# Turning the softmax weights of a sliding-window attention step in six 128-row blocks instead of eight

## The chip, the cores and the metric

The kernel runs on one core of one Trainium2 chip. The core has a matrix engine (TensorE, PE in the profile; its weight loads are listed apart as PEld), a vector engine (VectorE, DVE), a scalar engine (ScalarE, ACT), a general engine (GpSimd, POOL), queues that start transfers (SyncE, SP, and GpSimd's own), an on-chip memory of 128 partitions (SBUF) and accumulators for matrix products (PSUM, eight banks of 512 float32 per partition). Each engine takes its instructions in the order of its own list, and waits at an instruction until the others have signalled that its inputs are there. The metric is the device time of one execution in microseconds.

## The reference

One block of a streaming encoder: 1024 tokens of width 1024, in float32. A normed input is projected to queries, keys, values and several gates. Branch A is attention over a window of whole 64-token chunks, branch B a gated MLP; both are gated, summed and projected. What the change touches is the attention:

```python
# 16 query heads, 2 key heads, head width 64, chunks of 64 tokens
kb = concatenate([kc[:, j:j + nc] for j in range(3)], axis=2)   # a chunk sees its own and the two chunks before: 192 keys
s = einsum('bnqhgd,bnkhd->bhgnqk', qc, kb) * HEAD_DIM ** -0.5
s = where(valid, s, -1e30)
m = maximum(max(s, -1), sink)
p = exp(s - m)
denom = sum(p, -1) + exp(sink - m)                              # a learned sink per head
o = einsum('bhgnqk,bnkhd->bnqhgd', p / denom, vb)
```

The products are carried out on values split into a high and a low part (hi and lo), so that a product of two float32 matrices is three products of the parts.

## The kernel before, in words

Nearly all of the time goes to large products of 128x128 weights with 512 columns, written as a two-by-two scheme with seven products per pair of output blocks (`gemm_pair`, with the products issued at L338). A pair runs 7 x 12 matmuls; the weights of the next products are cast and split by ScalarE (L152) and VectorE (L153) in the meantime (`split_next`).

The attention has no time of its own. It is a generator (`attention`) of 32 steps: 2 key heads x 8 tiles of 128 tokens x 2 (`par`, the even or odd heads of the group's eight). After every product of the pairs that follow (`part_of_attention`, a hook) one piece of it is written into the program; the Tile scheduler then decides where each instruction stands in its engine's list. In the profile the steps lie between about 340 and 625 us.

A token tile holds two chunks, c = 0 and 1. Its keys are a block of 256: the 128 of the tile before and its own 128. Chunk 0 sees columns 0 to 191 of that block, chunk 1 columns 64 to 255. The four heads of a step are worked as two pairs (i = 0, 1), with the two heads' 64 queries in one set of 128 partitions. A step has three parts, issued in an interleaved way with those of other steps:

- `softmax_stage`: scores on PE (L1075) into one PSUM bank per chunk, their minimum on VectorE (L1083, L1084; scores carry a minus sign), the exponential on ScalarE into the tile `pr` (L1086), the sums' reciprocal (L1095 to L1099), and the scaling of the weights, chunk 0 on VectorE (L1105), chunk 1 on ScalarE (L1107).
- `weight_stage`, two steps later: the weights `pr` (queries on partitions) are turned by PE with the identity, so that the keys lie on partitions. For each of the four (c, i) the first 128 keys of the chunk's window go into one bank (L1127), then for each of the four its last 64 keys into another (L1138, 64 partitions). ScalarE copies a bank's high part (L152) and VectorE subtracts for the low part (L153): the first bank becomes `pT`, with high and low part side by side; the second becomes `pTb`, with the high part on partitions 0 to 63 and the low part on 64 to 127.
- `value_stage`, three steps after the softmax: the products with the values (L1160), per chunk two with `pT` and one with `pTb`, into a bank of kind `ps_o`; ScalarE copies (L1166) and VectorE adds (L1167) the halves into the tile `aT`, which is stored.

PSUM has four kinds of banks with two banks each: `ps_mm` and `ps_o` for the large products (`ps_o` also for the values), `ps_sc` for the scores and `ps_tp` for what is turned. The two banks of `ps_tp` are used in turn, so that a step's second bank can be written when the step before has read its own.

The values of a token tile are loaded by `value_loads` on SP's queue: two transfers (L988) bring the first 128 keys of each chunk's window into `va`, and two more (L991) the last 64 keys of both windows into `vb`, twice, since the high and the low part of the weights both need them. In the first token tile no keys lie before; it has its own case throughout.

Of the kernel before, what the change touches and what calls it, by code (L numbers as in the profile page):

```python
# [24 lines left out]
F32 = mybir.dt.float32  # L25
F32R = mybir.dt.float32r
# [4 lines left out]
P = 128  # L31
# [3 lines left out]
HALF = 512  # L35
# [17 lines left out]
def hybrid_tile(  # L53
# [16 lines left out]
    nc = tc.nc  # L70
# [8 lines left out]
    def nm(s):  # L79
        count[0] += 1  # L80
        return f"{s}_{count[0]}"

    def bank(tag, dt=F32):
        return psum.tile([P, 512], dt, name=nm("ps_" + tag), tag="ps_" + tag, bufs=2)

    def mtile(shape, dt, tag, bufs, pool=None):
        return (pool or main).tile(shape, dt, name=nm(tag), tag=tag, bufs=bufs)
# [13 lines left out]
    ident = const.tile([P, P], F32, name="ident")  # L101
# [43 lines left out]
    def split(hi, lo, src, minus=False):  # L145
        if minus:
            nc.scalar.mul(hi, src, -1.0)
            nc.vector.scalar_tensor_tensor(
                lo, src, -1.0, hi.bitcast(F32), op0=ALU.mult, op1=ALU.subtract
            )  # L150
        else:
            nc.scalar.copy(hi, src)  # L152
            return nc.vector.tensor_sub(lo, src, hi.bitcast(F32))  # L153
# [808 lines left out]
    keys = {}  # L962
# [10 lines left out]
    def value_loads(g, t):  # L973

        va = mtile([P, 2, 3 * HD], F32R, "v", 2, aheads)
        rows = v_dr[:].rearrange("n p g d -> (n p) g d")[:, g, :]
        if t == 0:
            for e in range(2):  # L980
                nc.sync.dma_start(va[e * 64 : (e + 1) * 64, 0, :].bitcast(F32), rows[0:64])
            nc.sync.dma_start(va[:, 1, :].bitcast(F32), rows[0:P])
            keys[g, t][1:3] = (None, va[:, 1, :]), (va[:, 0, :], None)
            return
        vb = mtile([P, 2, 3 * HD], F32R, "vb", 2, pool)
        for c in range(2):
            k = (t - 1) * P + 64 * c
            nc.sync.dma_start(va[:, c, :].bitcast(F32), rows[k : k + P])  # L988
        own = rows[t * P : (t + 1) * P].rearrange("(c p) d -> p c d", c=2)
        for e in range(2):  # L990
            nc.sync.dma_start(vb[e * 64 : (e + 1) * 64].bitcast(F32), own)  # L991
        keys[g, t][1:3] = (va[:, 0, :], va[:, 1, :]), (vb[:, 0, :], vb[:, 1, :])

    def query_stage(g, t, par):
        if par == 0:
# [57 lines left out]
    def atile(shape, dt, tag, bufs):  # L1053
        return mtile(shape, dt, tag, bufs, pool)

    def window_of(t, c):

        return (64 * c, 64 * c + 192) if t else (P, P + 64 * (c + 1))

    def softmax_stage(g, t, par, qt):  # L1060

        kt = keys[g, t][0]
        q_of = qt[:].rearrange("p i (q c) -> p c (i q)", c=2)
        k0 = 0 if t else P
        nmax = atile([P, 2, 2], F32, "sm", 12)
        sums = atile([P, 2, 2], F32, "sm", 12)
        pr = atile([P, 2, 2, 192], F32, "pr", 2)
        sinks_of = (v[:, 4 * g + par : 4 * g + par + 3 : 2] for v in (sink_sb, nsink_sb))
        sk, nsk = sinks_of
        for c in range(2):  # L1070
            lo, hi = window_of(t, c)
            sc = bank("sc")[:].rearrange("p (i k) -> p i k", i=2)
            for i in range(2):
                for f in range(2):
                    nc.tensor.matmul(  # L1075
                        sc[:, i, k0:],
                        q_of[:, c, i * P : (i + 1) * P],
                        kt[:, f, k0:],
                        start=f == 0,
                        stop=f == 1,  # L1080
                    )

            nc.vector.tensor_reduce(nmax[:, c, :], sc[:, :, lo:hi], axis=mybir.AxisListType.X, op=ALU.min)  # L1083
            nc.vector.tensor_tensor(nmax[:, c, :], nmax[:, c, :], nsk, op=ALU.min)  # L1084
            for i in range(2):
                nc.scalar.activation(  # L1086
                    pr[:, c, i, 0 : hi - lo],
                    sc[:, i, lo:hi],
                    AF.Exp,
                    bias=nmax[:, c, i : i + 1],  # L1090
                    scale=-1.0,
                    accum_out=sums[:, c, i : i + 1],
                )
        es = atile([P, 2, 2], F32, "sm", 12)
        nc.vector.tensor_add(es[:], sk.unsqueeze(1).broadcast_to([P, 2, 2]), nmax[:])  # L1095
        exps.append(nc.scalar.activation(es[:], es[:], AF.Exp))
        nc.vector.tensor_add(es[:], es[:], sums[:])
        inv = atile([P, 2, 2], F32, "sm", 12)
        nc.vector.reciprocal(inv[:], es[:])  # L1099
        for c in range(2):  # L1100
            lo, hi = window_of(t, c)
            for i in range(2):
                v = pr[:, c, i, 0 : hi - lo]
                if c == 0:
                    nc.vector.tensor_scalar_mul(v, v, inv[:, c, i : i + 1])  # L1105
                else:
                    nc.scalar.mul(v, v, inv[:, c, i : i + 1])  # L1107
        return pr

    def weight_stage(g, t, par, pr):  # L1110

        _, va, vb, _ = keys[g, t]

        def cols(c):
            return slice(256 * c, 256 * c + 256)

        a = b = None
        chunks = [c for c in range(2) if va[c] is not None]  # L1120
        if chunks:
            used = slice(256 * chunks[0], 512)
            pt = bank("tp")
            for c in chunks:
                for i in range(2):
                    at = (2 * c + i) * P
                    nc.tensor.transpose(pt[:, at : at + P], pr[:, c, i, 0:P], ident[:])  # L1127
            a = atile([P, 2, HALF], F32R, "pT", 2)
            split(a[:, 0, used], a[:, 1, used], pt[:, used])
        chunks = [c for c in range(2) if vb[c] is not None]  # L1130
        if chunks:
            used = slice(0, 256 * (chunks[-1] + 1))
            first = P if t else 0
            pt = bank("tp")
            for c in chunks:
                for i in range(2):
                    at = (2 * c + i) * P
                    nc.tensor.transpose(pt[0:64, at : at + P], pr[:, c, i, first : first + 64], ident[:])  # L1138
            b = atile([P, HALF], F32R, "pTb", 2)
            split(b[0:64, used], b[64:P, used], pt[0:64, used])  # L1140
        return a, b

    def value_stage(g, t, par, parts):


        if par == 0:
            keys[g, t][3] = atile([P, 4, P], F32, "aT", 2)
        _, va, vb, at = keys[g, t]
        a, b = parts
        po = bank("o")  # L1150
        vs = slice(par * HD, par * HD + P)
        for c in range(2):
            cs = slice(256 * c, 256 * c + 256)
            terms = []
            if va[c] is not None:
                terms += [(va[c][:, vs], a[:, n, cs]) for n in range(2)]
            if vb[c] is not None:
                terms.append((vb[c][:, vs], b[:, cs]))
            for n, (lt, rt) in enumerate(terms):
                nc.tensor.matmul(po[:, cs], lt, rt, start=n == 0, stop=n == len(terms) - 1)  # L1160
        here, there = slice(HD * par, HD * (par + 1)), slice(HD * (1 - par), HD * (2 - par))
        out_of, dst = (
            lambda half: po[half].rearrange("p (c i q) -> p c i q", c=2, i=4),
            at[here].rearrange("p i (c q) -> p c i q", c=2),
        )
        nc.scalar.copy(dst, out_of(there))  # L1166
        nc.vector.tensor_add(dst, dst, out_of(here))  # L1167
        if par == 1:
            nc.gpsimd.dma_start(
                at_dr[:].rearrange("(c p) t -> p c t", p=P)[:, 4 * g : 4 * g + 4, t * P : (t + 1) * P], at[:]  # L1170
            )

    def attention():
# [6 lines left out]
        def weigh(n):  # L1180
            weights.append(weight_stage(*steps[n], held.pop(0)))

        def value(n):
            value_stage(*steps[n], weights.pop(0))
            if n % 2 and n + 3 < len(steps):
                value_loads(*tiles[n // 2 + 2])
# [277 lines left out]
    def load_rows(p):  # L1464
        xr = mtile([P, 4, HALF], F32, "bq", 4, pool)
        for i in range(2):
            t = T_ORDER[p] + i
            copy_to(xr[:, 2 * i : 2 * i + 2, :].rearrange("p h n -> p (h n)"), x[t * P : (t + 1) * P, :])
        return xr
# [9 lines left out]
    rows = [load_rows(p) for p in range(3)]  # L1479
# [9 lines left out]
    for p in range(4):  # L1489
        n, t, acc, x11 = N_PAIRS + p, T_ORDER[p], accs[p], firsts[p]  # L1490
# [173 lines left out]
```

## Time and profile before

| | |
|---|---|
| runs | 939.69 us median of 3 (939.38 to 942.12) |
| profiled execution | 939.98 us, span 938.1 us, mean granted clock 0.996 |
| PE busy | 917.9 us (98%), 4525 matmuls |
| VectorE busy | 677.0 us (72%) |
| ScalarE busy | 531.6 us (57%) |
| GpSimd busy | 123.0 us (13%) |
| transfers | 201.60 MB, mean 215 GB/s |

The profile is one execution. "Busy" is the time in which an engine had an instruction running; matmuls overlap in the records, since the next one starts before the last one's end is recorded, so that the distance from start to start, not the recorded length, is what a matmul takes from its successor. In a row of a group, "x28 | 19.2, 684 | 1.1 <-ACT pTb" reads: 28 instructions, 19.2 us busy, 684 ns each, and the engine sat idle 1.1 us before them, mostly for that writer. In a row of waits, "2.1, 2, 1.2" is the sum, the number and the longest. In the timeline each row starts with the start and the length in us. The chain of waits goes back from the last instruction to whatever released it, step by step.

### The profile page before, as it was taken

The page shows a single profiled execution, that of the slowest core. Times are in us where ns is not written, and L with a number is a line of the kernel's source. Part 1 is how long each engine was busy: PE and PEld are TensorE (multiplying, and loading weights), DVE is VectorE, ACT ScalarE, POOL GpSimd, SP SyncE. Part 2 cuts the span into 40 slices and gives each one's busy share as a digit, 9 for nine tenths or more (in the row PEclk, how much of TensorE's full clock was granted, in tenths as well). Part 3 has the DMA queues.
Part 4 walks back from the last instruction along what each step waited for, and adds up shares of the span by engine and source line. Part 5 has one row for each costly group of instructions (what it writes and reads, how often), then busy time and mean ns, then how long its engine had stood idle before and what let it go on. Part 6 is the DMA issues. An engine that isn't in the chain of part 4 may idle for free.

```text
span 938.1 us, 13590 instructions
## 1 busy us (share of the span) xinstructions
PE 917.9 (98%) x4525; PEld 768.9 (82%) x4525; DVE 677.0 (72%) x1218; ACT 531.6 (57%) x1057; POOL 123.0 (13%) x199
## 2 busy tenths in 40 slices
PE   7999999999999999999999999999999999999996
PEld 6898888888888878888888888888887887888885
DVE  6755577665668678787878877756499489668996
ACT  7864343333445468777656676744475565457443
POOL 1211212221000001111111111101110011210012
PEclk9999999999999999999999999999999999999999
DMA  7343767888686778777777778859668754998622
GB/s 282 120 149 119 216 212 200 173 164 178 214 271 232 244 217 212 214 201 206 202 209 249 236 177 239 229 178 379 209 203 308 282 197 157 294 298 297 203 112 114
DMA packets 131301, 201.60 MB, mean 215 GB/s; under 512 B 12320, under 2 KB 64032, under 8 KB 131232
## 3 DMA queue, kind: packets, MB, share of 16 engines
q1 hardware_dynamic: 113616, 152.23, 49.0%
q0 software_dynamic: 17472, 48.24, 21.3%
q8 instruction: 36, 0.59, 0.3%
q14 instruction: 33, 0.27, 0.1%
q10 hardware_dynamic: 144, 0.26, 0.1%
HBM read 144.59 MB, written 85.46 MB: 245 GB/s over the span
## 4 chain that ended last, share of the span: by engine, by line
PE 75%; DVE 11%; ACT 5%; DMA 4%; issue 4%; SPq 1%; DVEq 0%; ACTq 0%
PE ps_mm L338 29%; PE ps_o L338 22%; PE ps_mm L624 6%; PE ps_tp L338 2%; PE ps_o L575 2%; PE ps_sc L1075 2%; PE ps_o L1160 2%; PE ps_sc L338 2%; DVE wl L153 2%; PE ps_tp L818 2%; ACT pr L1086 1%; DVE bq L182 1%; PE ps_tp L624 1%; PE ps_sc L624 1%; PE ps_o L624 1%
## 5 line engine op out<-in xcount | busy, mean ns | idle before, releaser
L152 ACT CAST wh<-s 128x1024 fp32r<-128x1024 f32 (+1 forms) x76 | 76.0, 1003 | 92.1 <-PE ps_mm L338 43.9
L153 DVE TENSOR_TENSOR wl<-wr,wh 128x1024 fp32r<-128x1024 f32 (+1 forms) x78 | 73.7, 947 | 53.6 <-ACT wh L152 52.9
L152 ACT CAST wh<-wr 128x1024 fp32r<-128x1024 f32 (+1 forms) x78 | 64.4, 829 | 80.4 <-PE ps_mm L338 33.7
L153 DVE TENSOR_TENSOR wl<-s,wh 128x1024 fp32r<-128x1024 f32 (+1 forms) x76 | 88.5, 1165 | 17.8 <-ACT wh L152 16.2
L1086 ACT ACTIVATE pr<-ps_sc,sm 128x192 f32<-128x192 f32 (+2 forms) x128 | 51.1, 410 | 35.6 <-DVE sm L1084 27.8
L338 PE MATMUL ps_o<-T_t1h,wh 128*128 128x512 f32 x144 | 57.1, 397 | 0.3 <-ACT wh L152 0.2
L338 PE MATMUL ps_o<-T_b22h,wh 128*128 128x512 f32 x144 | 57.2, 397 | 0.0
L338 PE MATMUL ps_o<-T_t1h,wl 128*128 128x512 f32 x144 | 56.3, 391 | 0.1
L338 PE MATMUL ps_o<-T_b22h,wl 128*128 128x512 f32 x144 | 56.2, 390 | 0.0
L338 PE MATMUL ps_o<-T_b22l,wh 128*128 128x512 f32 x144 | 56.1, 390 | 0.0
L338 PE MATMUL ps_o<-T_t1l,wh 128*128 128x512 f32 x144 | 56.1, 390 | 0.0
L338 PE MATMUL ps_mm<-T_b11h,wl 128*128 128x512 f32 x136 | 53.3, 392 | 2.0 <-DVE wl L153 2.0
L338 PE MATMUL ps_mm<-T_t3h,wh 128*128 128x512 f32 x136 | 54.1, 398 | 0.0
L338 PE MATMUL ps_mm<-T_t4h,wh 128*128 128x512 f32 x136 | 53.9, 396 | 0.0
L338 PE MATMUL ps_mm<-T_b11h,wh 128*128 128x512 f32 x136 | 53.7, 395 | 0.0
L338 PE MATMUL ps_mm<-T_t2h,wh 128*128 128x512 f32 x136 | 53.3, 392 | 0.2 <-ACT x L356 0.2
L338 PE MATMUL ps_mm<-T_t3l,wh 128*128 128x512 f32 x136 | 53.2, 391 | 0.0
L338 PE MATMUL ps_mm<-T_t3h,wl 128*128 128x512 f32 x136 | 53.2, 391 | 0.0
L338 PE MATMUL ps_mm<-T_t4h,wl 128*128 128x512 f32 x136 | 53.2, 391 | 0.0
L338 PE MATMUL ps_mm<-T_t2h,wl 128*128 128x512 f32 x136 | 53.0, 390 | 0.0
L338 PE MATMUL ps_mm<-T_b11l,wh 128*128 128x512 f32 x136 | 53.0, 390 | 0.0
L338 PE MATMUL ps_mm<-T_t4l,wh 128*128 128x512 f32 x136 | 53.0, 390 | 0.0
(374 smaller groups left out, 2474.8 us busy)
## 6 DMA issues: line engine op xcount, KB each, us to landing
wr<-in_w_dram SPq DMA_DIRECT2D x82, 256.0 KB
sums<-in_w_dram POOLq DMA_DIRECT2D x20, 512.0 KB, 5.3
s<-sums SPq DMA_DIRECT2D x20, 512.0 KB
s_dr<-x SPq DMA_DIRECT2D x32, 256.0 KB
q_hl<-qhl SPq DMA_DIRECT2D x16, 512.0 KB
q<-q_hl SPq DMA_DIRECT2D x64, 128.0 KB
wr<-in_w_dram SPq DMA_DIRECT2D x14, 512.0 KB
y_dr<-x POOLq DMA_DIRECT2D x28, 256.0 KB, 6.0
```

The costliest lines, as they stand in the source:

```text
L152: nc.scalar.copy(hi, src)
L153: return nc.vector.tensor_sub(lo, src, hi.bitcast(F32))
L182: op(dst[:, i : i + 2, :], a[:, i : i + 2, :], c[:, i : i + 2, :])
L338: nc.tensor.matmul(acc, lt, rt, start=fresh and k == 0 and n == 0, stop=k == 3 and n == 2, skip_group_check=True,)
L575: nc.tensor.matmul(acc[:, 0:256], lt[:, k, :], rt[:, k * 256 : (k + 1) * 256], start=j == 0 and k == 0 and n == 0, stop=j == 1 and k == 3 ...
L624: mm = nc.tensor.matmul(acc, lt, rt, start=k == 0 and n == 0, stop=k == KC - 1 and n == 2)
L818: nc.tensor.matmul(pm[:, t * P : (t + 1) * P], xh[:, half * 4 + t, g * P : (g + 1) * P], bias[-1][1][:, g % 4, :], start=True, stop=True,)
L1075: nc.tensor.matmul(sc[:, i, k0:], q_of[:, c, i * P : (i + 1) * P], kt[:, f, k0:], start=f == 0, stop=f == 1,)
L1086: nc.scalar.activation(pr[:, c, i, 0 : hi - lo], sc[:, i, lo:hi], AF.Exp, bias=nmax[:, c, i : i + 1], scale=-1.0, accum_out=sums[:, c, i : ...
L1160: nc.tensor.matmul(po[:, cs], lt, rt, start=n == 0, stop=n == len(terms) - 1)
```

## The change

The exponentials of a head pair's two chunks are now laid side by side in one row of 384 columns: chunk 0's 192 keys, then chunk 1's 192. Cut into blocks of 128, block 0 holds chunk 0's first 128 keys, block 2 chunk 1's last 128, and block 1 the 64 inner keys of both: chunk 0's last 64 and chunk 1's first 64. The outer blocks are turned as before, four transposes per step. The inner block is turned once per head pair, with 128 rows, so that there are two transposes where there were four; chunk 0 comes out on partitions 0 to 63, chunk 1 on 64 to 127. The high and low parts of that bank are made per chunk, two copies and two subtractions of 64x256 where there was one of each of 64x512, since chunk 1's high part now lies on partitions 64 to 127 and its low part on 0 to 63. What chunk 1 takes from the wide and from the narrow part changes with it: its last 128 keys are wide and its first 64 narrow. So `va` is the two 128-key blocks in order, loaded by one transfer, and `vb` the 64 keys on either side of the tile's start. The products with the values keep their number and size, and the first token tile keeps its work.

```diff
-        for c in range(2):
-            k = (t - 1) * P + 64 * c
-            nc.sync.dma_start(va[:, c, :].bitcast(F32), rows[k : k + P])
-        own = rows[t * P : (t + 1) * P].rearrange("(c p) d -> p c d", c=2)
+        k = t * P
+        nc.sync.dma_start(va[:].bitcast(F32), rows[k - P : k + P].rearrange("(c p) d -> p c d", c=2))
+        inner = rows[k - 64 : k + 64].rearrange("(c p) d -> p c d", c=2)
         for e in range(2):
-            nc.sync.dma_start(vb[e * 64 : (e + 1) * 64].bitcast(F32), own)
-        keys[g, t][1:3] = (va[:, 0, :], va[:, 1, :]), (vb[:, 0, :], vb[:, 1, :])
+            nc.sync.dma_start(vb[e * 64 : (e + 1) * 64].bitcast(F32), inner)
+        keys[g, t][1:3] = (va[:, 0, :], va[:, 1, :]), (vb[:, 1, :], vb[:, 0, :])
...
-        pr = atile([P, 2, 2, 192], F32, "pr", 2)
+        pr = atile([P, 2, 384], F32, "pr", 2)
+        held_in = {}
...
             for i in range(2):
+                at = 192 * c if t else P * (c + 1)
+                held_in[c, i] = pr[:, i, at : at + hi - lo]
                 nc.scalar.activation(
-                    pr[:, c, i, 0 : hi - lo],
+                    held_in[c, i],
...
-            pt = bank("tp")
-            for c in chunks:
-                for i in range(2):
-                    at = (2 * c + i) * P
-                    nc.tensor.transpose(pt[0:64, at : at + P], pr[:, c, i, first : first + 64], ident[:])
-            b = atile([P, HALF], F32R, "pTb", 2)
-            split(b[0:64, used], b[64:P, used], pt[0:64, used])
+        chunks = range(2 if t else 1)
+        rows = 64 * len(chunks)
+        pt = bank("tp")
+        for i in range(2):
+            turned(pt[0:rows, i * P : (i + 1) * P], i, 1, rows)
+        b = atile([P, 2, 256], F32R, "pTb", 2)
+        for c in chunks:
+            here, there = slice(64 * c, 64 * c + 64), slice(64 - 64 * c, P - 64 * c)
+            split(b[here, c, :], b[there, c, :], pt[here, 0:256])
...
-                terms.append((vb[c][:, vs], b[:, cs]))
+                terms.append((vb[c][:, vs], b[:, c, :]))
```

Here `turned(dst, i, block, width)` is `nc.tensor.transpose(dst, pr[:, i, block * P : block * P + width], ident[:])`; the outer blocks use it with blocks 0 and 2.

More of the change, by code (lines that the diff above doesn't have):

```diff
@@ L1100, in softmax_stage @@
         for c in range(2):
-            lo, hi = window_of(t, c)
             for i in range(2):
-                v = pr[:, c, i, 0 : hi - lo]
+                v = held_in[c, i]
                 if c == 0:
@@ L1110, in weight_stage, with turned @@
     def weight_stage(g, t, par, pr):
[L1114 to L1119, printed above, removed]
+        _, va, _, _ = keys[g, t]
+        def turned(dst, i, block, width=P):
+            nc.tensor.transpose(dst, pr[:, i, block * P : block * P + width], ident[:])
         chunks = [c for c in range(2) if va[c] is not None]
-        if chunks:
-            used = slice(256 * chunks[0], 512)
-            pt = bank("tp")
-            for c in chunks:
-                for i in range(2):
-                    at = (2 * c + i) * P
[L1127 to L1138, printed above, removed]
-            b = atile([P, HALF], F32R, "pTb", 2)
-            split(b[0:64, used], b[64:P, used], pt[0:64, used])
+        used = slice(256 * chunks[0], 512)
+        pt = bank("tp")
+        for c in chunks:
+            for i in range(2):
+                at = (2 * c + i) * P
+                turned(pt[:, at : at + P], i, 2 * c)
+        a = atile([P, 2, HALF], F32R, "pT", 2)
+        split(a[:, 0, used], a[:, 1, used], pt[:, used])
+        chunks = range(2 if t else 1)
+        rows = 64 * len(chunks)
+        pt = bank("tp")
+        for i in range(2):
+            turned(pt[0:rows, i * P : (i + 1) * P], i, 1, rows)
+        b = atile([P, 2, 256], F32R, "pTb", 2)
+        for c in chunks:
+            here, there = slice(64 * c, 64 * c + 64), slice(64 - 64 * c, P - 64 * c)
+            split(b[here, c, :], b[there, c, :], pt[here, 0:256])
         return a, b
```

## The prediction

> **What bounds the kernel now.** I read the page first (engines, then the chain), then the busy time by stretches of the attention stage, then the instructions that touch the turned weights, and last the timeline of single steps. The page:
>
> ```profile
> span 938.1 us, 13590 instructions
> ...
> PE 917.9 (98%) x4525; PEld 768.9 (82%) x4525; DVE 677.0 (72%) x1218; ACT 531.6 (57%) x1057; POOL 123.0 (13%) x199
> ...
> PE 75%; DVE 11%; ACT 5%; DMA 4%; issue 4%; SPq 1%; DVEq 0%; ACTq 0%
> ```
>
> TensorE (PE) is busy 98% of the span and carries 75% of the chain that ended last. The change only touches the stage in which the 32 attention steps run between the large products, from about 340 to 625 us, so the question is asked there again:
>
> ```profile
> 400.00:440.00 40.00, 39.99 (x222) 34.35 (x221) 31.85 (x69) 29.66 (x75) 4.99 (x6) 1.00 0.77 213
> ...
> 440.00:480.00 40.00, 38.96 (x214) 32.92 (x213) 32.25 (x76) 27.42 (x79) 6.36 (x8) 1.00 0.75 199
> ...
> 560.00:600.00 40.00, 40.00 (x223) 34.51 (x222) 31.44 (x72) 27.57 (x74) 4.94 (x6) 1.00 0.90 247
> ...
> sum 285.00, PE 281.90 PEld 240.14 DVE 221.72 ACT 200.25 POOL 37.18; mean PE 35.24 PEld 30.02 DVE 27.72 ACT 25.03 POOL 4.65
> ```
>
> The columns after the stretch are PE, weight loads, VectorE (DVE), ScalarE (ACT), GpSimd. PE is busy 281.9 of 285 us; VectorE has 63 us to spare, ScalarE 85 us. From 344 us on, what PE and its weight loads waited for in this stage is short:
>
> ```profile
> PE ps_o L338 <- DVE aT L1167: 2.1, 2, 1.2
> PE ps_mm L338 <- ACT x L356: 0.2, 1, 0.2
> ...
> PEld ps_o L338 <- DVE aT L1167: 4.0, 5, 1.4
> PEld ps_o L1160 <- DVE x L368: 1.9, 6, 0.5
> PEld ps_mm L338 <- ACT x L356: 0.6, 2, 0.4
> PEld ps_sc L1075 <- ACT pr L1086: 0.4, 1, 0.4
> PEld ps_mm L338 <- ACT x L363: 0.3, 1, 0.3
> ```
>
> All are banks of PSUM that a slower engine had still to empty; none is the turned weights or the values. So a PE instruction that goes is worth what it holds of PE, unless a bank is emptied later than now.
>
> **The change, part by part.** *Two transposes fewer in each of 28 steps* (32 steps, less the four of the first token tile, where two narrow ones stay). One step on PE:
>
> ```profile
> 566.14 0.28 PE L1160 MATMUL ps_o<-pTb,vb 128*128 128x256 f32 x1
> 566.26 0.60 PE L1127 MATMUL ps_tp<-ident,pr 128*128 128x128 f32 x4
> 566.70 0.60 PE L1138 MATMUL ps_tp<-ident,pr 128*64 128x128 f32 x4
> 567.05 0.48 PE L338 MATMUL ps_mm<-T_b11h,wh 128*128 128x512 f32 x1
> 567.37 0.40 PE L338 MATMUL ps_mm<-T_b11l,wh 128*128 128x512 f32 x1
> 567.60 0.40 PE L338 MATMUL ps_mm<-T_b11h,wl 128*128 128x512 f32 x1
> ```
>
> The first group of four starts 0.44 us before the second: 0.11 us each. The first product after the group starts early in the record and is 0.32 us ahead of its successor, where its successor keeps 0.23, so the eight are counted to there: (567.37 - 566.26 - 0.23) / 8 = 0.11 us. A narrow transpose (64 keys) holds PE as long as a wide one (both groups show 0.60 us), since 128 columns of the identity stream through in both, so the two that replace four cost the same each. I take the finer 0.109 us of a start-to-start in the trace: 28 x 2 x 0.109 = 6.1 us less on PE. Bounds: nothing, if PE is not what ends the stage, and the whole duration of a record, next.
>
> ```profile
> L1138 PE MATMUL ps_tp<-ident,pr x120: 272/273/421, 341.4 to 617.3; 128*64 128x128 f32 x120
> ```
>
> A record lasts 0.273 us, of which 0.16 lie under the next one's; 56 x 0.273 = 15.3 us is the upper end. I take 6.1, because the starts are what the next instruction sees. The Trainium skill, "TensorE: Matmul & The Clock Gate", section "Part 4: PE-mode transpose", gives about 275 ns for a transpose in a kernel's context; by that as the price the sum would fall by 15.4 us. The trace agrees with it as a record's length and differs as a price.
>
> *The narrow weights are split in two pieces.* Instead of one copy (ScalarE) and one subtraction (VectorE) of 64x512 there are two of each of 64x256. The first token tile shows the smaller ones already:
>
> ```profile
> L153 DVE TENSOR_TENSOR pTb<-ps_tp,pTb 64x512 fp32r<-64x512 f32 x28 | 19.2, 684 | 1.1 <-ACT pTb L152 0.2
> L152 ACT CAST pTb<-ps_tp 64x512 fp32r<-64x512 f32 x28 | 16.2, 580 | 0.0
> ...
> L153 DVE TENSOR_TENSOR pTb<-ps_tp,pTb 64x256 fp32r<-64x256 f32 x4 | 1.7, 418 | 0.1
> L152 ACT CAST pTb<-ps_tp 64x256 fp32r<-64x256 f32 x4 | 1.5, 372 | 0.0
> ```
>
> ScalarE: 28 x (2 x 0.372 - 0.580) = 4.6 us more; VectorE: 28 x (2 x 0.418 - 0.684) = 4.3 us more. Against the spare 85 and 63 us that is hidden; without cover it would be at most 8.9 us, and it cannot be a gain.
>
> *A new wait.* In the changed program's instruction list the second copy waits for VectorE: both chunks now lie in one bank, and the first chunk's subtraction reads that bank before the second copy may. So the four pieces run in turn: copy, subtraction, copy, subtraction. Whatever stands behind the second copy in ScalarE's list waits with it: exps, casts of the products' weights, the copies that empty banks. The subtraction can be quick or far off:
>
> ```profile
> 560.96 0.56 ACT L152 CAST pTb<-ps_tp 64x512 fp32r<-64x512 f32 x1
> 561.55 0.69 DVE L153 TENSOR_TENSOR pTb<-ps_tp,pTb 64x512 fp32r<-64x512 f32 x1 [0.21 <-ACT pTb L152]
> ...
> 525.14 0.58 ACT L152 CAST pTb<-ps_tp 64x512 fp32r<-64x512 f32 x1
> ...
> 527.52 0.69 DVE L153 TENSOR_TENSOR pTb<-ps_tp,pTb 64x512 fp32r<-64x512 f32 x1
> ```
>
> From the end of the first small copy to the end of the first small subtraction that is 0.6 us (561.97 - 561.33) in the one step and 2.4 us (527.94 - 525.51) in the other. In most steps the changed list has other ScalarE work between the two copies (a cast, exps, an emptied bank), so part of this is filled; in seven the copies are neighbours. The consumers are far away:
>
> ```profile
> 571.52 0.68 DVE L153 TENSOR_TENSOR pTb<-ps_tp,pTb 64x512 fp32r<-64x512 f32 x1
> ...
> 577.48 0.60 PE L1138 MATMUL ps_tp<-ident,pr 128*64 128x128 f32 x4
> ...
> 583.96 0.50 PE L1160 MATMUL ps_o<-pT,v 128*128 128x256 f32 x2
> ...
> 413.33 0.68 DVE L153 TENSOR_TENSOR pTb<-ps_tp,pTb 64x512 fp32r<-64x512 f32 x1
> ...
> 414.83 0.60 PE L1138 MATMUL ps_tp<-ident,pr 128*64 128x128 f32 x4
> ```
>
> In the first pair the weights are ready at 572.2 and used at 583.96, 11.8 us later; their bank is written again at 577.48, 5.3 us later. A delay of one or two microseconds is covered there. The second pair is the tight one: the bank is free at 414.01 and written at 414.83; in the changed list two products stand between the wide and the narrow transposes of a step in this part, which gives half a microsecond back. What is not covered is a bank that is late already: the waits above came 18 times. If each grows by the 0.15 us that a step gains on either engine, that is 2.7 us; most of them are weight loads that lie beside a running product, so I take a third, 0.9 us.
>
> *The order of the narrow transposes.* They now need both chunks' scaled weights; before, two of the four did too, and the group was emptied as one. No cost. *Values loaded by one transfer instead of two* per token tile: 14 issues fewer on SP's queue, the same bytes. No row above waits for it; worth nothing, and if its data were late, the value products (L1160) would wait, which now wait only for a bank (1.9 us). *The products themselves* keep count and size.
>
> **Sum.** The profiled execution took 939.98 us (span 938.1). 939.98 - 6.1 + 0.9 = 934.8. The median of the runs, 939.69, is 0.3 lower, so I forecast 934.5 us.
>
> **Rivals.** (1) *The new wait decides, slower.* Place: ScalarE between the two copies, with the copy of the head outputs (aT) or of a product's quarter (x) behind it, and PE waiting for that bank, as it already does for aT. The change breaks even where each of the 28 steps loses 2 x 0.109 = 0.22 us on PE. With 0.5 us, a third of the middle between 0.6 and 2.4, it gives 28 x 0.5 - 6.1 = +7.9, 947.6 us. For it: three steps have aT right behind the second copy. Against: ScalarE's 85 spare us, and PE's waits are 9.5 us in all today. The Trainium skill, "PSUM — Partial Sum Buffer", section "PSUM bank collisions raise a hardware error", says that two engines may touch one bank at once where the partitions lie in different quadrants, as the two chunks' rows 0-63 and 64-127 do; by it the wait would not be needed, but the program makes it, and no row of before shows such a pair. (2) *PE's gain is not passed on.* The stage is paced by the softmax relay between VectorE, ScalarE and PE (16% of the chain), and the 6.1 us become idle time of PE: 939.98 - 6.1 + 6.1, less the 0.3, 939.7 us. Against: PE's 281.9 of 285. (3) *A transpose costs its whole record:* 939.98 - 15.3 - 0.3 = 924.4 us. Against: the starts, 0.11 us apart.
>
> **Chances.** Forecast 0.79 (own range 932.8 to 936.8: no new stall at all gives 933.6; the growth of all waits gives 936.3). Rival 1: 0.11. Rival 2: 0.08. Rival 3: 0.02. A measurement tells 0.3% (2.8 us) from no change. Faster by more than that, below 936.9: 0.80; within: 0.09; slower: 0.11. The range of 932.5 to 939.8 takes in the forecast and most of rival 2.
>
> **What would show it.** Right: the narrow transposes as a group of two with 128 rows, 0.22 us from start to next; the 64x256 pieces at 0.37 and 0.42 us; PE still near 99% busy in a stage that ends about 5 us earlier; the later stages unchanged. Wrong: PE or its weight loads waiting longer for aT or x (rival 1), a growing ScalarE wait on pTb with PE idle behind it; or PE's busy share in the stage falling by 2% with the same end (rival 2).

## The result, and the profile after

The changed kernel takes 942.86 us (median of 12 runs, 941.17 to 945.32) where the kernel before takes 939.66 us beside it: 1.0034 times as long, 95% interval 1.0023 to 1.0045. It is slower by some 3.2 us, against a forecast of 934.5 us.

The page of the changed kernel, its engines and its chain:

```profile
span 940.9 us, 13537 instructions
...
PE 913.7 (97%) x4469; PEld 763.5 (81%) x4469; DVE 684.6 (73%) x1246; ACT 536.8 (57%) x1085; POOL 123.2 (13%) x199
...
PE 73%; DVE 12%; DMA 6%; ACT 5%; issue 3%; SPq 1%; ACTq 0%; DVEq 0%
```

PE has 56 matmuls fewer and is busy 4.2 us less, and yet the span is 2.8 us longer: PE stands idle more. The stretches of the attention stage, with the columns as before:

```profile
400.00:440.00 40.00, 39.07 (x215) 33.35 (x213) 32.05 (x74) 31.79 (x82) 5.01 (x6) 1.00 0.76 213
440.00:480.00 40.00, 37.50 (x200) 31.30 (x199) 33.36 (x78) 26.88 (x80) 6.38 (x8) 1.00 0.72 187
...
560.00:600.00 40.00, 39.44 (x218) 33.84 (x217) 32.09 (x78) 28.73 (x84) 4.10 (x5) 1.00 0.93 248
```

In the stretch from 440 us PE was idle 1.0 us before and is idle 2.5 us now; from 400 and from 560 us it was never idle, and loses 0.9 and 0.6 us. What PE itself (without its weight loads) waited for from 344 us on, in the changed kernel:

```profile
PE ps_o L338 <- DVE aT L1168: 4.5, 4, 1.6
PE ps_o L1161 <- DVE x L368: 1.4, 4, 0.6
PE ps_mm L338 <- ACT x L356: 1.1, 2, 0.7
PE ps_mm L338 <- ACT x L363: 1.0, 1, 1.0
PE ps_tp L1122 <- DVE pTb L153: 0.7, 2, 0.5
PE ps_o L1161 <- DVE aT L1168: 0.5, 1, 0.5
```

That is 9.2 us where it was 2.3 us, all of it for banks that ScalarE or VectorE had still to empty. The narrow pieces themselves, over the stage, and the first waits of ScalarE:

```profile
L153 DVE TENSOR_TENSOR pTb<-ps_tp,pTb 64x256 fp32r<-64x256 f32 x60 | 25.3, 422 | 2.7 <-ACT pTb L152 0.9
L152 ACT CAST pTb<-ps_tp 64x256 fp32r<-64x256 f32 x60 | 22.1, 368 | 20.6 <-DVE pTb L153 20.3
```

```profile
ACT pTb L152 <- DVE pTb L153: 20.3, 18, 3.7
ACT pr L1091 <- DVE sm L1087: 19.1, 18, 1.8
```

The second copy of a step waits for VectorE's first subtraction, 20.3 us in all and up to 3.7 us at a time; this wait did not exist before. One step in the timeline shows how it reaches PE:

```profile
546.87 0.37 ACT L152 CAST pTb<-ps_tp 64x256 fp32r<-64x256 f32 x1
...
547.75 0.42 DVE L153 TENSOR_TENSOR pTb<-ps_tp,pTb 64x256 fp32r<-64x256 f32 x1
...
548.20 0.56 DVE L1086 TENSOR_REDUCE sm<-ps_sc 128x2 f32<-128x384 f32 x1
548.21 0.37 ACT L152 CAST pTb<-ps_tp 64x256 fp32r<-64x256 f32 x1 [0.96 <-DVE pTb L153]
...
548.79 0.43 DVE L153 TENSOR_TENSOR pTb<-ps_tp,pTb 64x256 fp32r<-64x256 f32 x1
...
549.25 0.16 DVE L1087 TENSOR_TENSOR sm<-sm,nsink_sb 128x2 f32<-128x2 f32 x1
...
549.50 0.42 ACT L1091 ACTIVATE pr<-ps_sc,sm 128x192 f32<-128x192 f32 x1 [0.93 <-DVE sm L1087]
...
552.65 0.58 ACT L1167 COPY aT<-ps_o 64x512 f32<-64x512 f32 x1
...
553.26 0.69 DVE L1168 TENSOR_TENSOR aT<-aT,ps_o 64x512 f32<-64x512 f32 x1 [0.94 <-ACT aT L1167]
...
554.00 0.50 PE L338 MATMUL ps_o<-T_b21h,wh 128*128 128x512 f32 x1 [1.58 <-DVE aT L1168]
```

ScalarE waits 0.96 us for the first subtraction. VectorE has the second subtraction in its list between the first score minimum (L1086) and the comparison with the sink (L1087) that the exponentials wait for, so the first of the four exponentials starts at 549.50. The copy and the addition of the head outputs (aT), which stand behind the four, end at 553.95. PE needs that bank and stands idle for 1.58 us. In the kernel before, PE has no wait at this product, which starts 1.02 us behind the product before it (549.65 and 550.67); here it is 2.63 us (551.37 and 554.00). In copies_first, an experiment below in which no copy waits for VectorE, PE is idle 0.3 us there.

Not all of the 1.58 us is this one wait. VectorE came late to the step already: its subtraction for pT starts 1.6 us behind PE's product of 545.42, and 0.9 us behind the same product in copies_first. Nor does every stall of PE come from the wait. The one of 1.02 us for a product's quarter (x, L363) is still 0.74 us in copies_first, and 0.83 us in two_transposes_out, which has six transposes and the single copy of before.

### The profile page after: what moved, and what is told of

Read it like the earlier page. It is cut to its first block, busy times and chain, and to the rows that moved or that the text cites. A ratio compares the mean times of both kernels' runs of the same rounds, so it can differ in the third digit from the quotient of the medians.

```text
span 940.9 us, 13537 instructions
## 1 busy us (share of the span) xinstructions
PE 913.7 (97%) x4469; PEld 763.5 (81%) x4469; DVE 684.6 (73%) x1246; ACT 536.8 (57%) x1085; POOL 123.2 (13%) x199
## 4 chain that ended last, share of the span: by engine, by line
PE 73%; DVE 12%; DMA 6%; ACT 5%; issue 3%; SPq 1%; ACTq 0%; DVEq 0%
PE ps_mm L338 29%; PE ps_o L338 22%; PE ps_mm L624 6%; PE ps_sc L338 2%; PE ps_tp L338 2%; PE ps_o L575 2%; DVE wl L153 2%; ACT pr L1091 2%; PE ps_sc L1078 2%; PE ps_tp L818 2%; PE ps_o L1161 1%; DMA q<-q_hl 1%; PE ps_tp L1122 1%; PE ps_tp L624 1%; PE ps_sc L624 1%
```

## The experiments

Three explanations stood beside each other at first: the new wait (W), the fixed cost of the added instructions (F), and that PE's saving is not passed on at all (N). Each ratio is to the kernel before, run beside it on the same chip, with its interval. The stage is that of the profiled execution, from the start of the first transpose of weights to the start of the last product with values; before it is 280.4 us, at a mean granted clock of 0.996 for the whole execution. The last column has that clock for the others: where it differs, the stages differ by more than the edit.

| kernel | ratio (95%) | stage, us | clock |
|---|---|---|---|
| changed kernel | 1.0034 (1.0023 to 1.0045) | 282.7 | 0.995 |
| copies_first | 0.9999 (0.9986 to 1.0013) | 280.0 | 0.996 |
| split_in_turn | 1.0087 (1.0072 to 1.0103) | 288.6 | 0.994 |
| split_copies_first | 1.0013 (0.9996 to 1.0029) | 280.9 | 0.996 |
| two_transposes_out | 0.9958 (0.9943 to 0.9974) | 276.6 | 0.997 |
| out_and_copies_first | 0.9958 (0.9945 to 0.9971) | 276.2 | 0.996 |
| two_loads | 0.9999 (0.9985 to 1.0014) | 280.8 | 0.996 |
| second_from_64 | 1.0010 (0.9997 to 1.0023) | 281.8 | 0.992 |
| second_from_0 | 0.9983 (0.9967 to 1.0000) | 276.9 | 0.996 |
| late_split | 0.9968 (0.9955 to 0.9982) | 280.3 | 0.993 |
| late_narrow_split | 0.9976 (0.9964 to 0.9988) | 278.0 | 0.995 |
| before_late_split | 0.9998 (0.9985 to 1.0011) | 281.7 | 0.994 |

**copies_first.** Only the order of the four pieces changes, and with it the wait.

```diff
-        for c in chunks:
-            here, there = slice(64 * c, 64 * c + 64), slice(64 - 64 * c, P - 64 * c)
-            split(b[here, c, :], b[there, c, :], pt[here, 0:256])
+        here = [slice(64 * c, 64 * c + 64) for c in range(2)]
+        for c in chunks:
+            nc.scalar.copy(b[here[c], c, :], pt[here[c], 0:256])
+        for c in chunks:
+            nc.vector.tensor_sub(b[here[1 - c], c, :], pt[here[c], 0:256], b[here[c], c, :].bitcast(F32))
```

> The changed kernel with the four pieces of the inner block in another order: both copies, then both subtractions, so that no copy waits for VectorE; the instructions are the same. Theory W (the new wait of ScalarE on VectorE cost the 9 us): the wait of 20.3 us is gone and the gain of the transposes comes through, 934 to 936 us. Theory F (the fixed cost of one more instruction per step on ScalarE and on VectorE): no better than the changed kernel, 942 to 944 us. Theory N (PE's saving is not passed on, the softmax relay paces the stage): 939 to 943 us.

Measured 941.43 us against 941.48 beside it, ratio 0.9999. ScalarE no longer waits for VectorE at the copies. The loss of the changed kernel is gone, so the order of the pieces cost it 0.35%; the gain of the transposes did not come (W asked for 934 to 936 us, and 941.43 lies where N had it), so W was not all of it. F is ruled out as the cause of the slowdown: the instructions are the same and the time is not.

**split_in_turn** and **split_copies_first** put the two pieces into the kernel before, with its eight transposes and its layout.

```diff
-            split(b[0:64, used], b[64:P, used], pt[0:64, used])
+            for c in chunks:
+                piece = slice(256 * c, 256 * c + 256)
+                split(b[0:64, piece], b[64:P, piece], pt[0:64, piece])
```

> The kernel before with its eight transposes, but the narrow bank split in two pieces of 64x256 in turn: copy, subtraction, copy, subtraction. Theory W: PE keeps its work and gets the stalls, 939.7 + 9 = 949 us. Theory F: also 949 us, and the same as with both copies first. Theory N: 942 to 944 us, about as the changed kernel.

```diff
-            split(b[0:64, used], b[64:P, used], pt[0:64, used])
+            pieces = [slice(256 * c, 256 * c + 256) for c in chunks]
+            for piece in pieces:
+                nc.scalar.copy(b[0:64, piece], pt[0:64, piece])
+            for piece in pieces:
+                nc.vector.tensor_sub(b[64:P, piece], pt[0:64, piece], b[0:64, piece].bitcast(F32))
```

> The kernel before with its eight transposes and the narrow bank split in two pieces, both copies first and then both subtractions. Theory W: 940 to 941 us, next to nothing. Theory F: 949 us, as with the pieces in turn. Theory N: 942 to 944 us.

In turn: 1.0087, 8.2 us slower. Both copies first: 1.0013, with an interval that reaches to no change. The instructions are the same, so the wait costs 0.74%, 7.0 us, in this layout, and the extra instructions next to nothing. The first waits of ScalarE in split_in_turn:

```profile
ACT pTb L152 <- DVE pTb L153: 23.2, 16, 3.7
```

**two_transposes_out** takes PE's part of the change alone: two narrow transposes of a step are left out and the bank's 256 columns are read twice by the same copy and subtraction, so that one chunk's 64 inner keys stand in for the other's.

```diff
-            for c in chunks:
-                for i in range(2):
-                    at = (2 * c + i) * P
-                    nc.tensor.transpose(pt[0:64, at : at + P], pr[:, c, i, first : first + 64], ident[:])
+            for i in range(2):
+                nc.tensor.transpose(pt[0:64, i * P : (i + 1) * P], pr[:, chunks[-1], i, first : first + 64], ident[:])
...
-            split(b[0:64, used], b[64:P, used], pt[0:64, used])
+            n = len(chunks)
+            twice = pt[0:64, 0:256].unsqueeze(1).broadcast_to([64, n, 256])
+            hi, lo = (b[rows, used].rearrange("p (c q) -> p c q", c=n) for rows in (slice(0, 64), slice(64, P)))
+            split(hi, lo, twice)
```

> The kernel before with two of the four narrow transposes of a step left out (the 64 inner keys of one chunk are read twice from the bank, so chunk 0's last 64 keys get chunk 1's weights; the rest of the work is kept). This is PE's saving by itself. Theories W and F: 939.7 - 6.1 = 933.6 us, 932.5 to 935. Theory N: 939 to 940 us.

Measured 0.9958, 4.0 us faster, between N and the rest: the interval, 0.9943 to 0.9974, excludes the whole 6.1 us (0.9935) as well as no change. From start to start, the transposes follow one another for 23.0 us in the stage of the kernel before and for 16.7 us here (16.8 in the changed kernel): the saving on PE is there. Some 2 us go back, and the waits show where: PE comes sooner to banks that ScalarE and VectorE have still to empty. Its waits:

```profile
PE ps_o L338 <- DVE aT L1168: 4.0, 4, 2.1
PE ps_mm L338 <- ACT x L363: 0.8, 1, 0.8
PE ps_mm L338 <- ACT x L356: 0.5, 1, 0.5
PE ps_o L1161 <- DVE x L368: 0.3, 1, 0.3
```

PE waits 5.6 us here where it waited 2.3 us before. The copy and the subtraction that read the bank twice take what they took (0.580 and 0.684 us), so they are not the cause.

**out_and_copies_first** joins the two parts that had no loss, and **two_loads** gives copies_first its two value transfers back. With copies_first 2.7 us behind what its parts add up to (-0.42% and +0.13%), either the parts do not add (I), or something in the new layout costs (A). The first diff is against two_transposes_out, the second against copies_first.

```diff
...
-            split(hi, lo, twice)
+            pieces = [slice(256 * c, 256 * c + 256) for c in chunks]
+            for piece in pieces:
+                nc.scalar.copy(b[0:64, piece], pt[0:64, 0:256])
+            for piece in pieces:
+                nc.vector.tensor_sub(b[64:P, piece], pt[0:64, 0:256], b[0:64, piece].bitcast(F32))
```

> The kernel before with two narrow transposes of a step left out (one chunk's 64 inner keys are read twice) and the narrow bank split in two pieces, both copies first: PE's saving and the extra pieces, without the new layout of the weights and values. Apart they measured -0.42% and +0.13%. Theory A (the two effects add, and what copies_first lost beside them comes from the new layout: narrow transposes that need both chunks, one transfer for the values): -0.29%, some 2.7 us under before. Theory I (they do not add: a PE that runs ahead meets banks emptied later): as copies_first, 0.0%, within 0.15%.

```diff
-        nc.sync.dma_start(va[:].bitcast(F32), rows[k - P : k + P].rearrange("(c p) d -> p c d", c=2))
+        for c in range(2):
+            nc.sync.dma_start(va[:, c, :].bitcast(F32), rows[k + (c - 1) * P : k + c * P])
```

> copies_first, with the values of a token tile loaded by two transfers again instead of one. Theory A with the transfer as the cause: some 2 to 3 us faster than copies_first. Theory I, or A with the layout of the weights as the cause: the same as copies_first within 0.15%.

0.9958 and 0.9999: the parts do not get in each other's way (their sum is 0.9971, the end of the interval), so theory I falls, and the single transfer is free. So 0.4% lies in what copies_first has beyond out_and_copies_first. The instruction lists of ScalarE and VectorE are the same in the two, in kind, shape and order. The rows of the pieces are not. In copies_first, two copies and two subtractions of a step:

```profile
510.83 0.75 ACT L1141 CAST pTb<-ps_tp 64x256 fp32r<-64x256 f32 x2
...
512.25 0.86 DVE L1143 TENSOR_TENSOR pTb<-ps_tp,pTb 64x256 fp32r<-64x256 f32 x2
```

and in out_and_copies_first, in the same step:

```profile
509.59 0.64 ACT L1140 CAST pTb<-ps_tp 64x256 fp32r<-64x256 f32 x2
...
510.98 0.75 DVE L1142 TENSOR_TENSOR pTb<-ps_tp,pTb 64x256 fp32r<-64x256 f32 x2
```

A single piece takes 0.37 and 0.42 us in both. Where both pieces start on partition 0, the second begins before the first has ended (0.263 us from start to start on ScalarE, 0.342 on VectorE, medians of 27 and 26 pairs); where the second starts on partition 64 it waits for the end (0.378 and 0.431 us).

**second_from_64** and **second_from_0** test that alone. Both have 128-key transposes of one chunk's weights, so that the bank has 128 rows; they differ in where the second piece is read and written, and both keep the layout of before, so that one chunk's keys stand in for the other's. The diff is against out_and_copies_first.

```diff
-                nc.tensor.transpose(pt[0:64, i * P : (i + 1) * P], pr[:, chunks[-1], i, first : first + 64], ident[:])
+                nc.tensor.transpose(
+                    pt[0:rows, i * P : (i + 1) * P], pr[:, chunks[-1], i, begin : begin + rows], ident[:]
+                )
...
+            here = [slice(0, 64), slice(64, P)]      # second_from_0: slice(0, 64)
+            there = [slice(64, P), slice(0, 64)]     # second_from_0: slice(64, P)
...
+                nc.scalar.copy(b[here[c], 256 * c : 256 * c + 256], pt[here[c], 0:256])
...
+                nc.vector.tensor_sub(b[there[c], piece], pt[here[c], 0:256], b[here[c], piece].bitcast(F32))
```

> out_and_copies_first with the narrow transposes 128 keys wide and the second piece of the narrow bank read from partitions 64 to 127 (its high part written there, its low part on 0 to 63), as the changed kernel has it; weights and values keep the layout of before, so one chunk's keys stand in for the other's. Theory P (a piece that starts on partition 64 behind one that starts on 0 does not overlap with it, 0.38 us from start to start on ScalarE and 0.43 on VectorE where it was 0.26 and 0.34, and PE's waits grow by it): as copies_first, 0.0% against before, within 0.15%. Theory B (narrow transposes that need both chunks' scaled weights, which this kernel does not have): -0.4%, as out_and_copies_first.

> The control: the same 128-key transposes, but both pieces read from partitions 0 to 63. Theory P: -0.4%, as out_and_copies_first, with 0.26 and 0.34 us from start to start. Theory B: -0.4% too. A theory that the 128 rows of the transposes cost it: 0.0%, the same as second_from_64.

1.0010 and 0.9983 on the same chip, 0.27% apart where theory P, the start partition, asked for 0.4%. The two intervals just touch (0.9997 and 1.0000 at their ends), but each carries the noise of the kernel before; the twelve runs of the one and the twelve of the other have means 3.1 us apart, with a 95% interval of 1.4 to 4.9 us. The lists of ScalarE and VectorE are again the same in the two. Starts are 0.377 and 0.431 us apart with the second piece from 64, and 0.263 and 0.342 from 0. PE's own waits are 6.3 us (3.0 aT, 1.9 x of ScalarE, 1.2 other values' banks, 0.2 pTb) against 4.9. The stage of the profiled executions is 281.8 against 276.9 us; an estimate from the granted clock, 0.85 against 0.92 from 340 to 360 us and 0.96 against 1.00 from 440 to 480, puts 2 to 3 us of that down to the clock, since part of the first stretch lies ahead of the stage. Theory B falls, since these kernels' narrow transposes need one chunk only and second_from_64 still loses.

second_from_0 stays short of the -0.4% that was expected of it, with -0.17%. Its stage is as long as that of out_and_copies_first (276.9 and 276.2 us), so the 128 rows of the transposes show no cost there. By the ratios, taken on two chips, it is 0.25% behind, and 0.4 us at the same granted clock (the last section), so that a cost of the rows is not excluded. So the start on 64 is shown as a cause, and that it is all of the 0.4% is not: what may be left for the new layout stays within the intervals.

**late_split**, **late_narrow_split** and **before_late_split.** If late exponentials are what makes banks late, the pieces should stand behind the softmax piece in the lists. In late_split both banks of copies_first are emptied there, in late_narrow_split only the narrow one; before_late_split does the former in the kernel before.

```diff
         def weigh(n):
-            weights.append(weight_stage(*steps[n], held.pop(0)))
+            turned_of.append(weight_stage(*steps[n], held.pop(0)))   # transposes only; returns the function that empties the banks
...
             held.append(softmax_stage(*step, qT.pop(0)))
+            part()                                                   # now the copies and subtractions
```

> copies_first, with the copies and subtractions of both banks (pT and pTb) written behind the softmax piece of the same turn instead of ahead of it, so that the score minima and the exponentials stand ahead of them in the lists of VectorE and ScalarE. If what remains is that these pieces delay the exponentials and with them the banks that PE waits for (theory I), the stalls shrink: 935 to 938 us, 0.4% under before. If the pieces' place does not matter: as copies_first. If the two banks that are then held longer matter more: slower, 943 us or above.

> The kernel before, eight transposes, with the splits of both banks written behind the softmax piece. Control for late_split: if the place of the splits is a gain by itself, 1 to 3 us under before; if PE's later work was the reason that they hurt, no change; if the banks held longer matter, slower.

> late_split with only the narrow bank's pieces behind the softmax piece; the wide bank is emptied as early as before. If the gain of late_split (-0.32%) comes from the narrow pieces: -0.3% or better, 937 to 939 us. If it comes from the wide ones: as copies_first, 0.0%.

0.9968, 0.9998 and 0.9976. Six transposes with the pieces behind the softmax beat both kernels: late_split takes 938.09 us against 940.92 beside it, 0.32% less (0.18 to 0.45%), a little short of the 0.4% expected. In the kernel before, the place makes no difference, and moving the narrow pieces alone gives a gain of the same size within the intervals. The traces agree that the exponentials are the link. Count from one and the same product of PE, for each step the last one ahead of its exponentials in the kernel before. The step's last exponential ends 1.80 us behind that product in the kernel before (median of 32 steps), 2.51 us in copies_first, 2.61 in the changed kernel, and 1.69 and 1.74 in late_split and late_narrow_split. In before_late_split they come early too (1.57 us), but there was little to gain: PE waits 2.5 us there and 2.3 before. What PE waits for in late_narrow_split:

```profile
PE ps_tp L1122 <- DVE pTb L1146: 1.7, 2, 1.5
PE ps_o L338 <- DVE aT L1175: 1.5, 2, 1.2
PE ps_mm L338 <- ACT x L356: 1.1, 2, 0.6
PE ps_o L1168 <- DVE x L368: 0.2, 1, 0.2
```

aT is down to 1.5 us from the 3.0 of copies_first (4.5 in the changed kernel), and the price of the late pieces is visible as the wait for pTb, 1.7 us where copies_first has 0.6.

## Why the prediction was wrong

- *The saving on PE: right in size.* 6.1 us were forecast, and the starts show 6.2 us less. The narrow transposes of 128 rows hold PE as long as those of 64, 0.109 us, and rival 3, a transpose at its whole record, is out.
- *"If each grows by the 0.15 us that a step gains on either engine, that is 2.7 us; ... I take a third, 0.9 us": the step that failed.* The new wait was seen, with the two cases of 0.6 and 2.4 us, and priced by the length of the added instructions. Its price is what stands behind it. In the layout of before it costs 7.0 us alone (split_in_turn against split_copies_first), in the changed one 0.35%, 3.3 us (the changed kernel against copies_first). The slack that was quoted, 11.8 us from the turned weights to their use, was true and beside the point: it covers the consumers of the pieces, not the exponentials and the emptied banks that queue behind them on ScalarE and VectorE. These had less slack: at 554.00 PE was idle for 1.58 us where it had no wait before.
- *That the pieces are hidden: right for their number, wrong for their place, the second step that failed.* Two pieces on the same partitions cost 0.13% with an interval that reaches to nothing. That the second one starts on partition 64 was put at nothing. It costs 0.27% where it was tried alone, and copies_first misses out_and_copies_first by 0.4%.
- *That a saving on PE is passed on whole:* 4.0 of 6.1 us were, so rival 2, given 0.08, holds for a third of the saving.
- *Sum.* The forecast was 5.2 us under before and the result is 3.2 over, 8.4 us apart. Along the runs: -3.9 us with the saving and free pieces (out_and_copies_first), -0.1 with the changed layout (copies_first), +3.2 with the pieces in turn. So 2.2 us went with what was not passed on of the saving (3.9 of 6.1), 3.8 with the start on 64 and what else the layout costs, and 2.4 with the wait, 3.3 where 0.9 was forecast. Taken in another order the shares differ: out_and_copies_first with the 7.0 us of the wait in the layout of before gives +3.1 us at once, as if the start on 64 cost nothing once the pieces are in turn. It may add little there, since the wait already keeps the two pieces of an engine apart, but that was not tried, and the agreement with 3.2 is partly luck.
- *Rival 1, given 0.11, had the direction and the place right,* and its point of decision (0.22 us per step). A stall of 0.5 us per step was its price, for the wait alone. The stage lost 2.3 + 6.2 = 8.5 us, 0.30 us per step; 6.9 us of it are waits of PE itself (9.2 less 2.3), and taking the new wait out leaves PE with 6.7 us of them (copies_first). The evidence against it, 85 us of spare ScalarE time and waits of 9.5 us in all, was an average over the stage and did not speak of what is late where.
- *The single value transfer and the new dependence of the narrow transposes:* free, as said; two_loads measured the first. The second was not tried alone, but second_from_64, which lacks it, is no faster than copies_first (1.0010 and 0.9999).

## What to carry to other kernels

A wait put into the middle of an engine's list can cost what stands behind it in that list, and not only what depends on the waiting instruction: before pricing one, look which emptied banks follow it and when PE next writes them. Where an engine copies and another subtracts from the same bank in pieces, write all copies first and all subtractions after; with six transposes it also paid to write them behind the softmax. And a saving on the busiest engine can be worth less than its length where others free its buffers, 4.0 of 6.1 us here: measure it by leaving the work out before building the layout that saves it.

## What the runs showed of the hardware

*Two pieces that start on partitions 0 and 64 do not overlap.* VectorE: 0.342 us from start to start with both reads from partition 0, 0.431 with the second from 64. The Trainium skill, "VectorE: DVE Perf Modes", section "Two Vector instructions with no wait between them", says that an instruction whose input or output starts in another group of 32 partitions than the last one's is held until all earlier ones have finished; the traces agree, 0.431 us being the length of a piece (0.42) and a little. ScalarE does the same here, 0.263 against 0.378 us.

*The spread between runs goes with the clock that was granted.* The 87 runs of the kernel before beside the later experiments lie between 937.4 and 944.7 us; those with a mean clock of 0.998 have a median of 939.1 us (7 runs), of 0.996 940.7 (43), of 0.994 942.5 (17): nearly 1 us per 0.001. Over all 206 runs there, one straight line in the clock for all kernels together gives 0.9 us per 0.001, and at the same clock late_split stands 4.4 us under the kernel before (plus or minus 0.6), out_and_copies_first 3.8, second_from_0 3.4, second_from_64 0.9, copies_first 0.7. That is a fit over three chips, and the clock may itself follow from the waits. Some drops of the clock stand behind idle time of PE: in the profile of late_split PE is idle 0.9 us between 384 and 388 us, and the next two stretches of 4 us are granted 0.66 and 0.91 of the clock:

```profile
384.00:388.00 4.00, 3.08 (x16) 2.35 (x14) 2.46 (x7) 2.89 (x11) 0.00 (x0) 1.00 1.05 270
388.00:392.00 4.00, 3.12 (x8) 2.35 (x9) 3.91 (x8) 2.48 (x7) 2.46 (x4) 0.66 0.92 262
392.00:396.00 4.00, 4.00 (x21) 3.47 (x20) 3.00 (x5) 1.05 (x1) 0.88 (x2) 0.91 1.02 246
```

Others do not: in the changed kernel PE is busy for only 2.42 of the 4 us from 552 us, and the next two stretches are granted 1.00. If idle time is a cause of drops, which was not tried alone, some stalls cost more than their length; comparisons of less than 0.2% need many runs, or the clock beside them.
